# A diffusion trunk's modulation products in eight pair steps, and two of four value bands loaded later

## Chip, core and metric

The kernel runs on one core of a Trainium2 chip. The metric is device time in microseconds (us) of one execution; lower is better. Three runs of the kernel before gave a median of 1276.81 us (1274.63 to 1281.95). Engines are called as the profile calls them: PE (TensorE matmul; PEld is its weight load), DVE (VectorE), ACT (ScalarE), POOL (GpSimd) and SP (SyncE), whose queue issues every DMA of this kernel, in program order.

## What is computed

Two layers over 1152 tokens (128 context, 1024 latent on a 16 x 64 grid), width 1024. Each layer normalizes, modulates by a shift and a scale, mixes, and adds the result back through a gate:

```python
x = x + gate * mixer(rmsnorm(x) * (1 + scale) + shift)
(shift, scale, gate) = silu(cond) @ w_mod[l] + b_mod[l]
```

The even layer's mixer is a gated linear recurrence (HGRN2, 4 heads) beside a neighbourhood attention (8 heads of width 64, window 8 x 16, a relative bias, and all context keys); the odd layer's is a convolution with a gated recurrence. The change concerns the middle of the even layer: the projections that make keys, queries and gates of the attention, beside which the kernel computes the modulation rows that are needed later (layer 0's gate, layer 1's shift, scale and gate).

## The kernel before

Weights and activations are float32, split into a high and a low fp32r part; a product is three matmuls (high x high, low x high, high x low).

**Units.** `unit_f(i, c)` multiplies weight block `i` (128 output columns) by chunk `c` (384 tokens): 8 x 3 = 24 matmuls (L316 to L318) into one PSUM tile. The attention's projections (the loop over `p`, `n`, `c` at the end of the listing) are 12 weight blocks, block 3p + n, with three units each: **units 0 to 35**, block b being units 3b to 3b + 2. For n = 0 a unit's result goes to the keys, for n = 1 to the queries (tile `kq`), for n = 2 to the gate (`yT`). ACT copies each out of PSUM (helper `act`, L77), the gate with a DVE step behind it (L365). PSUM tag `mm` has three buffers, so unit u + 3 can't start before unit u's tile has been read.

**Weights.** `w_get(i, 0, 1)` splits block `i + 1` while block `i` is used: the load `wraw` (512 KB), its high part on ACT (`wh`, 1.06 us), its low part on POOL (`wl`, L186). A `wh` stands in ACT's order between two units' copies: while it waits for its load, the copies behind it wait as well.

**Modulation.** The later modulation is two groups of 8 blocks of k. One block is 1 MB of `w_mod` (two tiles `wm`) and four matmuls (L221), one for each column group of 32, that accumulate into one PSUM tile. After the 8th block DVE adds the bias row (`modR`, L227); `mod_done` transposes it (L234), sets the factors and stores the gate row (`gate_d`).

**What sets the order.** `at(u, f, ...)` puts a call on an agenda, and `tick()`, called after each unit, runs what stands there for that unit. Tile's scheduler then makes each engine's order from priorities and free buffers. Large tiles (`wm`, `wraw`, `wh`, `wl`, `kq`, `vband`, ...) share 20 buffers of one pool, `slab`. A load is issued when SP comes to it, its buffer is free, and the load eight places before it on SP has landed.

**Bands.** The values were stored to `vb_d` in DRAM before the stage. `band_load(Rg)` brings four grid rows back as keys for the attention: four loads `vband` of 256 KB whose access pattern has 4 as its outermost size. Bands 0 to 2 are read by the first half's items, bands 1 to 3 by the second's. Behind the bands SP issues six masks (`mkt`), the cached keys and values (`kc`, `vc`) and the biases (`bT`, outermost size 8); POOL and DVE subtract a bias from a mask (`nbm`, L822), and the first score of the attention (PE L845, then DVE L852) needs the first of these.

Of the kernel before, what the change touches and what calls it, by code (L numbers as in the profile page):

```python
# [33 lines left out]
def trunk_kernel(ctx: ExitStack, tc: tile.TileContext, x, wm0, wm, bmr, wfe, wv, woe, wfo, woo, rgw, sm, st0,  # L34
# [12 lines left out]
    def slab(name, shape=(128, T), dt=F32):  # L47
        return sp.tile(list(shape), dt, name=name, tag="slab")
# [3 lines left out]
    def psum(tag, shape=(128, 512)):  # L52
        return pp.tile(list(shape), F32, name="ps_" + tag, tag=tag, bufs=PB[tag])

    def load(out, in_):
        return nc.sync.dma_start(out=out, in_=in_)
# [139 lines left out]
    def w_get(i, la_load, la_split):  # L196
        w_split(i)
        w_split(i + la_split)
        w_load(i + la_load)
        return split[i]  # L200


    rows = {}

    def mod_load(g, ks):
        for k in ks:
            for hf in range(2):
                t = slab("wm", (128, 1024))
                load(t, wm[g - 1, k, :, hf * 1024:(hf + 1) * 1024])
                rows[g, k, hf] = t  # L210

    def mod_row(g):
        t = slab("bmrow", (128, 512))
        ap = bass.AP(tensor=bmr.tensor, offset=bmr.offset + g * 2048, ap=[[512, 4], [0, 32], [1, 512]])
        load(t, ap)
        return t

    def mod_mm(g, ps, ks):
        for k in ks:
            for b in range(4):  # L220
                PE.matmul(ps[32 * b:32 * b + 32, :], condS[:, k, :],  # L221
                          rows[g, k, b // 2][:, (b % 2) * 512:(b % 2 + 1) * 512],
                          start=(k == 0), stop=(k == 7), skip_group_check=True)

    def mod_evac(g, ps, bm):
        R = slab("modR", (128, 512))
        V.tensor_tensor(R, ps, bm, OP.add)  # L227
        return R
# [118 lines left out]
    def at(u, f, *a):  # L347
        agenda.setdefault(u, []).append((f, a))
# [359 lines left out]
    def vb_unit(b, t):  # L708
        o = unit_v(IVB + 2 * b, t)
        if t == 0:  # L710
            dst = vbc[:, b * 256:(b + 1) * 256]
        else:
            if (t - 1) // 2 not in vbt:
                vbt[(t - 1) // 2] = slab("vbt", (128, 2, 512))
            dst = vbt[(t - 1) // 2][:, (t - 1) % 2, b * 256:(b + 1) * 256]
        with tc.high_priority(200):
            act(dst, o, AF.Copy)
        tick()

    def band_store(Rg):  # L720
        store(vb_d[2 * Rg:2 * Rg + 2].rearrange("t p f -> p t f"), vbt.pop(Rg))
# [10 lines left out]
    for b in range(2):  # L732
        w_get(IVB + 2 * b + 1, 2, 1)
        for t in range(9):
            if b == 1 and t in (2, 5, 8):
                mod_load(1, [t // 3])
            vb_unit(b, t)
            if t == 5:
                w_get(IVB + 2 * b + 1, 2, 2)
            if b == 1 and t in (2, 4, 6, 8):  # L740
                band_store(t // 2 - 1)
        split.pop(IVB + 2 * b)
        split.pop(IVB + 2 * b + 1)
# [2 lines left out]

    mst = {}

    MODS = [(g, k) for g in (1, 2) for k in range(8)]

    def mod_step(n):
        g, k = MODS[n]
        if k == 0:
            mst["ps"] = psum("a")
        mod_mm(g, mst["ps"], [k])
        rows.pop((g, k, 0))
        rows.pop((g, k, 1))
        if n + 3 < len(MODS):
            mod_load(MODS[n + 3][0], [MODS[n + 3][1]])
        if k == 7:  # L760
            mst[g] = mod_evac(g, mst["ps"], mod_row(g))

    def mod_done(g):
# [148 lines left out]
            V.tensor_tensor(yT[4 + p, 0][:, 0:128], o[:, 0:128], yT[4 + p, 0][:, 0:128], OP.mult)  # L912

    U = clock["u"]
    for n in range(16):
        at(U + 4 + n, mod_step, n)
        if n % 8 == 7:
            at(U + 4 + n + 1, mod_done, MODS[n][0])
    for Rg in range(4):
        at(U + 20 + 3 * Rg, band_load, Rg)  # L920
    for p in range(4):
        for n in range(3):
            i = IP + 3 * p + n
# [30 lines left out]
    for i in range(n_it + 3):  # L954
        if 0 <= i - 2 < n_it:
            a_trans(i - 2)
        if i < n_it:
            a_score(i)
            p, hf, j = items[i]
# [23 lines left out]
    def out_tiles(i0, ts, last=8, cuts=HALVES):  # L983

        ps = {t: [psum("o" if n == 1 and p else "mm") for p in cuts[:-1]] for n, t in enumerate(ts)}
        for ks in (range(last), range(last, 8)):
            for t in ts:
                c, tt = divmod(t, 3)
                z = slice(tt * 128, (tt + 1) * 128)
                for o, p, q in zip(ps[t], cuts, cuts[1:]):  # L990
                    for k in ks:
                        yh, yl = ysp[k, c]
                        wh, wl = split[i0 + k]
                        PE.matmul(o[:, :q - p], yh[:, z], wh[:, p:q], start=(k == 0), stop=False)  # L994
                        PE.matmul(o[:, :q - p], yh[:, z], wl[:, p:q], start=False, stop=False)  # L995
                        PE.matmul(o[:, :q - p], yl[:, z], wh[:, p:q], start=False, stop=(k == 7))  # L996
        return ps
# [19 lines left out]
    for t in range(9):  # L1017
        xt = slab("xt", (128, 1024))
        load(xt, x[t])
        ps = out_tiles(IWE, [t])[t]  # L1020
# [195 lines left out]
    for pos in range(max(ev) + 1):  # L1216
# [6 lines left out]
        n, c = seq[pos]  # L1223
# [14 lines left out]
    for t in range(9):  # L1238
# [3 lines left out]
        ps = pst[t] if t < 2 else out_tiles(IWO, [t], 8, cuts)[t]  # L1242
# [128 lines left out]
```

## Time and profile before

| | us |
|---|---|
| median of three runs | 1276.81 |
| the profiled execution's own time | 1281.0 |
| its span | 1279.2 |
| PE busy | 1204.3 (94%) |
| DVE busy | 680.5 (53%) |
| ACT busy | 529.2 (41%) |
| POOL busy | 349.1 (27%) |

PE is busy nearly throughout, so a gap on PE or a stretch at a lower clock is what lengthens the span; the other engines matter where PE waits for them. The profile lists for a stretch the busy time of each engine, the clock granted to PE (1.00 is 2.4 GHz, 0.50 is 1.2 GHz), the mean busy share of the 16 DMA engines and GB/s; in a timeline, `[4.21 <-DVE yT L365]` is idle time before an instruction and what ended it. The profiled execution is 4.2 us above the median.

### The profile page before, as it was taken

To read this page: it belongs to the slowest core of one execution; us is meant where nothing else is said; L and a number is where in the kernel's file an instruction comes from. 1 tells how busy PE (TensorE), PEld (TensorE's weight loads), DVE (VectorE), ACT (ScalarE), POOL (GpSimd) and SP (SyncE) were. 2 spreads that over 40 slices of the span, in tenths; PEclk is the share of its full clock that TensorE was granted. 3 is DMA by queue.
4 is the path that set the end of the run, shared out by engine and by line. 5 is a ranking of instruction groups with operands and counts; after the bars stand their busy time and mean duration, and the time that the engine had idled before them with its cause. 6 is when DMAs were issued, how large, how long until landed. Compare 5 with 4: busy or idle time off the path is not lost. (4 is left out here: it accounts for less than half of the span.)

```text
span 1279.2 us, 19143 instructions
## 1 busy us (share of the span) xinstructions
PE 1204.3 (94%) x7536; PEld 1082.4 (85%) x7536; DVE 680.5 (53%) x1424; ACT 529.2 (41%) x1057; POOL 349.1 (27%) x261
## 2 busy tenths in 40 slices
PE   5999998999999999998999999999988999898897
PEld 3889998999999997787956667888988999897686
DVE  5547128314555200000168996654678779888744
ACT  3435134323343211111146674323477586574311
POOL 0142032421505110111150420025444435442000
PEclk9999999999998999998969999999989999999899
DMA  9510100111010446522430224223011111112432
GB/s 349 194 34 22 34 17 26 36 52 37 18 40 25 155 165 210 199 84 100 128 120 2 98 83 181 99 100 132 17 34 46 46 28 39 42 53 64 139 124 83
DMA packets 41909, 110.45 MB, mean 86 GB/s; under 512 B 4180, under 2 KB 14804, under 8 KB 41820
## 3 DMA queue, kind: packets, MB, share of 16 engines
q1 hardware_dynamic: 41820, 109.24, 25.1%
q8 instruction: 59, 0.97, 0.3%
q14 instruction: 30, 0.25, 0.1%
HBM read 96.61 MB, written 12.61 MB: 85 GB/s over the span
## 5 line engine op out<-in xcount | busy, mean ns | idle before, releaser
L316 PE MATMUL ps_mm<-hTh,wh 128*128 128x384 f32 x936 | 320.1, 346 | 11.2 <-DVE yT L365 4.2
L317 PE MATMUL ps_mm<-hTl,wh 128*128 128x384 f32 x936 | 319.8, 342 | 2.3 <-DVE hTl L307 1.7
L318 PE MATMUL ps_mm<-hTh,wl 128*128 128x384 f32 x936 | 319.9, 342 | 1.0 <-POOL wl L186 1.0
L186 POOL TENSOR_TENSOR wl<-wraw,wh 128x1024 fp32r<-128x1024 f32 x48 | 123.5, 2574 | 285.9 <-ACT wh L77 251.1
L316 PEld LDWEIGHTS ps_mm<-hTh,wh 128*128 128x128 f32 x936 | 177.6, 191 | 27.4 <-ACT kq L77 7.0
L317 PEld LDWEIGHTS ps_mm<-hTl,wh 128*128 128x128 f32 x936 | 178.4, 191 | 4.6 <-DVE hTl L307 3.3
L318 PEld LDWEIGHTS ps_mm<-hTh,wl 128*128 128x128 f32 x936 | 178.4, 191 | 1.8 <-POOL wl L186 1.6
L994 PE MATMUL ps_mm<-wh,yh 128*128 128x512 f32 (+1 forms) x288 | 112.8, 393 | 6.1 <-ACT yh L77 5.8
L995 PE MATMUL ps_mm<-wl,yh 128*128 128x512 f32 (+1 forms) x288 | 113.1, 393 | 2.0 <-DVE wl L186 2.0
L996 PE MATMUL ps_mm<-wh,yl 128*128 128x512 f32 (+1 forms) x288 | 112.5, 391 | 1.7 <-DVE yl L977 1.7
L77 ACT ACTIVATE wh<-wraw 128x1024 fp32r<-128x1024 f32 x68 | 71.4, 1057 | 86.5 <-DMA wraw<-in_wfe_dram 39.7
L339 PE MATMUL ps_mm<-wh,hTh 128*128 128x256 f32 x288 | 83.2, 289 | 2.0 <-ACT va L77 2.0
L341 PE MATMUL ps_mm<-wh,hTl 128*128 128x256 f32 x288 | 81.9, 284 | 0.0
L340 PE MATMUL ps_mm<-wl,hTh 128*128 128x256 f32 x288 | 81.8, 284 | 0.0
L262 POOL TENSOR_TENSOR ss<-ss,nhalf 128x1 f32<-128x1 f32 x27 | 15.2, 564 | 243.8 <-DVE ss L261 186.2
L1127 POOL TENSOR_TENSOR yT<-yT,rt 128x384 f32<-128x384 f32 x42 | 56.8, 1382 | 72.2 <-DVE rt L1124 72.2
L77 ACT ACTIVATE res<-xt 128x512 f32<-128x512 f32 (+1 forms) x37 | 22.9, 619 | 124.9 <-DVE xt L1004 117.0
L994 PEld LDWEIGHTS ps_mm<-wh,yh 128*128 128x128 f32 x288 | 54.6, 190 | 18.6 <-ACT yh L77 6.3
L822 POOL TENSOR_TENSOR nbm<-mkt,bT 128x384 f32<-128x384 f32 x42 | 44.8, 1084 | 86.9 <-DMA bT<-in_bias_dram 51.7
L995 PEld LDWEIGHTS ps_mm<-wl,yh 128*128 128x128 f32 x288 | 54.5, 189 | 15.8 <-DVE wl L186 4.1
L996 PEld LDWEIGHTS ps_mm<-wh,yl 128*128 128x128 f32 x288 | 54.5, 189 | 13.7 <-DVE yl L977 2.3
L365 DVE SCALAR_TENSOR_TENSOR yT<-yT,ps_mm 128x384 f32<-128x384 f32 x10 | 5.5, 554 | 113.2 <-ACT yT L77 113.2
(258 smaller groups left out, 2458.5 us busy)
## 6 DMA issues: line engine op xcount, KB each, us to landing
wm<-in_wm_dram SPq DMA_DIRECT2D x48, 512.0 KB
wraw<-in_wfe_dram SPq DMA_DIRECT2D x28, 512.0 KB
xt<-in_x_dram SPq DMA_DIRECT2D x18, 512.0 KB
bT<-in_bias_dram SPq DMA_DIRECT2D x48, 192.0 KB
wraw<-in_wfo_dram SPq DMA_DIRECT2D x16, 512.0 KB
x_d<-xt SPq DMA_DIRECT2D x9, 512.0 KB
xt<-x_d SPq DMA_DIRECT2D x9, 512.0 KB
out_dram<-xt SPq DMA_DIRECT2D x18, 256.0 KB
```

The lines of the kernel that those rows point to most:

```text
L77: i = A.activation(out, in_, func, **kw)
L186: (lo_eng or G).tensor_tensor(lo, r, hi.bitcast(F32), OP.subtract)
L316: PE.matmul(o, w1, hh, start=(k == 0), stop=False)
L317: PE.matmul(o, w1, hl, start=False, stop=False)
L318: PE.matmul(o, w2, hh, start=False, stop=(k == 7))
L339: PE.matmul(o, hh, w1, start=(k == 0), stop=False)
L340: PE.matmul(o, hh, w2, start=False, stop=False)
L341: PE.matmul(o, hl, w1, start=False, stop=(k == 7))
L994: PE.matmul(o[:, :q - p], yh[:, z], wh[:, p:q], start=(k == 0), stop=False)
L995: PE.matmul(o[:, :q - p], yh[:, z], wl[:, p:q], start=False, stop=False)
L996: PE.matmul(o[:, :q - p], yl[:, z], wh[:, p:q], start=False, stop=(k == 7))
L1127: G.tensor_tensor(us[c], us[c], r[:, c * CW:(c + 1) * CW], OP.mult)
```

## The change

The 16 steps of one block become 8 steps of two blocks, at every second unit from unit 4 on (4, 6, ..., 18) in place of every unit from 4 to 19. Loads run two pairs ahead (8 `wm` tiles) where they ran three blocks ahead (6 tiles), so four blocks, not three, are loaded before the stage. `mod_done` of the second group comes one unit earlier. Bands 2 and 3 are put on the agenda at units 33 and 34 in place of 26 and 29; bands 0 and 1 stay at 20 and 23.

```diff
@@ -732,8 +732,8 @@
-            if b == 1 and t in (2, 5, 8):
-                mod_load(1, [t // 3])
+            if b == 1 and t in (2, 4, 6, 8):
+                mod_load(1, [t // 2 - 1])
@@ -746,18 +746,19 @@
-    MODS = [(g, k) for g in (1, 2) for k in range(8)]
+    MODS = [(g, (k, k + 1)) for g in (1, 2) for k in (0, 2, 4, 6)]
 
     def mod_step(n):
-        g, k = MODS[n]
-        if k == 0:
+        g, ks = MODS[n]
+        if n % 4 == 0:
             mst["ps"] = psum("a")
-        mod_mm(g, mst["ps"], [k])
-        rows.pop((g, k, 0))
-        rows.pop((g, k, 1))
-        if n + 3 < len(MODS):
-            mod_load(MODS[n + 3][0], [MODS[n + 3][1]])
-        if k == 7:
+        mod_mm(g, mst["ps"], ks)
+        for k in ks:
+            for hf in range(2):
+                rows.pop((g, k, hf))
+        if n + 2 < len(MODS):
+            mod_load(*MODS[n + 2])
+        if n % 4 == 3:
             mst[g] = mod_evac(g, mst["ps"], mod_row(g))
@@ -912,12 +913,12 @@
-    for n in range(16):
-        at(U + 4 + n, mod_step, n)
-        if n % 8 == 7:
-            at(U + 4 + n + 1, mod_done, MODS[n][0])
+    for n in range(8):
+        at(U + 4 + 2 * n, mod_step, n)
+        if n % 4 == 3:
+            at(U + 4 + 2 * n + 1, mod_done, MODS[n][0])
     for Rg in range(4):
-        at(U + 20 + 3 * Rg, band_load, Rg)
+        at(U + (20, 23, 33, 34)[Rg], band_load, Rg)
```

Three places show how the scheduler's order moves.

PE, behind unit 4, the first step. Before:

```order
L317 MATMUL ps_mm<-hTl,wh 128x384
L318 MATMUL ps_mm<-hTh,wl 128x384
L221 MATMUL ps_a<-wm,condS 32x512 x4
L316 MATMUL ps_mm<-hTh,wh 128x384
L317 MATMUL ps_mm<-hTl,wh 128x384
```

and now:

```order
L317 MATMUL ps_mm<-hTl,wh 128x384
L318 MATMUL ps_mm<-hTh,wl 128x384
L221 MATMUL ps_a<-wm,condS 32x512 x8
L316 MATMUL ps_mm<-hTh,wh 128x384
L317 MATMUL ps_mm<-hTl,wh 128x384
```

The four matmuls of the second block have come up from behind unit 5 and stand directly behind those of the first; the same at the other seven steps.

SP, from the weights of block 8 to the first masks (the difference; `out_dram<-kq` are the stores of the new keys of p = 2 and p = 3):

```order
+L59 DMA out_dram<-kq 128x128
 L56 DMA wraw<-in_wfe_dram 128x1024
 L56 DMA vband<-vb_d 128x1x512 x4
-L56 DMA wraw<-in_wfe_dram 128x1024
-L56 DMA vband<-vb_d 128x1x512 x4
-L56 DMA wraw<-in_wfe_dram 128x1024
-L56 DMA vband<-vb_d 128x1x512 x4
+L56 DMA wraw<-in_wfe_dram 128x1024 x3
 L59 DMA out_dram<-kq 128x128
-L56 DMA wraw<-in_wfe_dram 128x1024
+L56 DMA vband<-vb_d 128x1x512 x8
 L56 DMA mkt<-in_msk_dram 128x384 x6
```

The loads of blocks 9, 10 and 11 now stand together behind band 1; bands 2 and 3 stand behind them and behind the store of p = 3's keys (unit 27), directly ahead of the masks. In the program's text the bands are called at units 33 and 34; in SP's order nothing of unit 28 or later stands ahead of them.

ACT, units 20 to 30, from the keys' last copy of p = 2 on. Before:

```order
L77 ACTIVATE kq<-ps_mm 128x384 x3
L77 ACTIVATE wh<-wraw 128x1024
L77 ACTIVATE kq<-ps_mm 128x128
L77 ACTIVATE kq<-ps_mm 128x4x4x16 x2
L77 ACTIVATE kq<-ps_mm 128x2x4x16
L77 ACTIVATE wh<-wraw 128x1024
L77 ACTIVATE kq<-ps_mm 128x6x4x16
L77 ACTIVATE yT<-ps_mm 128x384
L77 ACTIVATE wh<-wraw 128x1024
L77 ACTIVATE yT<-ps_mm 128x384 x2
```

and now:

```order
L77 ACTIVATE kq<-ps_mm 128x384 x2
L77 ACTIVATE wh<-wraw 128x1024
L77 ACTIVATE kq<-ps_mm 128x384
L77 ACTIVATE kq<-ps_mm 128x128
L77 ACTIVATE kq<-ps_mm 128x4x4x16 x2
L77 ACTIVATE kq<-ps_mm 128x2x4x16
L77 ACTIVATE wh<-wraw 128x1024
L77 ACTIVATE kq<-ps_mm 128x6x4x16
L77 ACTIVATE wh<-wraw 128x1024
L77 ACTIVATE yT<-ps_mm 128x384 x3
```

The high part of block 8 has moved ahead of unit 20's copy (it stood behind it), that of block 9 stays between the copies of units 22 and 23, and that of block 10 has moved from behind unit 24's copy to ahead of it.

## Rows read from the trace of the kernel before

**Rows 1.** The page's first line: the profiled execution.

```profile
span 1279.2 us, 19143 instructions
```

**Rows 2.** Stretches: length; busy PE, PEld, DVE, ACT, POOL (instructions); granted clock, DMA share, GB/s.

```profile
475.56:557.81 82.25, 82.25 (x493) 65.15 (x492) 4.19 (x8) 12.77 (x24) 12.02 (x5) 1.00 0.51 172
557.81:594.28 36.47, 34.55 (x200) 33.71 (x196) 1.48 (x4) 4.24 (x9) 4.80 (x2) 1.00 0.36 119
594.28:598.66 4.38, 0.17 (x1) 0.00 (x0) 0.61 (x2) 2.07 (x4) 0.94 (x1) 0.91 0.09 36
598.66:605.69 7.03, 7.03 (x24) 7.03 (x25) 0.41 (x1) 0.12 (x1) 1.47 (x1) 0.57 0.18 58
```

**Rows 3.** Waits of PE, 560 to 606 us: total, times, longest.

```profile
PE ps_mm L316 <- DVE yT L365: 4.2, 1, 4.2
PE ps_mm L316 <- ACT kq L77: 1.6, 1, 1.6
PE ps_mm L318 <- POOL wl L186: 0.3, 1, 0.3
```

**Rows 4.** Timeline of SP's queue: start, duration of the issue, DMA.

```profile
559.31 1.71 SPq L56 DMA_DIRECT2D vband<-vb_d  x3
561.12 0.62 SPq L56 DMA_DIRECT2D wraw<-in_wfe_dram  x1
...
571.32 0.90 SPq L56 DMA_DIRECT2D wraw<-in_wfe_dram  x1
...
583.58 2.40 SPq L56 DMA_DIRECT2D wraw<-in_wfe_dram  x1
600.15 2.58 SPq L56 DMA_DIRECT2D vband<-vb_d  x4
...
605.52 19.10 SPq L56 DMA_DIRECT2D mkt<-in_msk_dram  x6
...
629.11 10.88 SPq L56 DMA_DIRECT2D bT<-in_bias_dram  x14
```

**Rows 5.** Timeline of ACT: start, duration, instruction [idle before, what ended it].

```profile
572.21 1.06 ACT L77 ACTIVATE wh<-wraw 128x1024 fp32r<-128x1024 f32 x1 [9.44 <-DMA wraw<-in_wfe_dram]
...
584.31 1.06 ACT L77 ACTIVATE wh<-wraw 128x1024 fp32r<-128x1024 f32 x1 [10.16 <-issue]
...
596.59 1.06 ACT L77 ACTIVATE wh<-wraw 128x1024 fp32r<-128x1024 f32 x1 [10.46 <-DMA wraw<-in_wfe_dram]
```

**Rows 6.** Timeline of PE: two steps and the unit between; a unit without one.

```profile
475.56 1.07 PE L221 MATMUL ps_a<-wm,condS 128*32 128x512 f32 x8
...
476.01 0.61 PE L221 MATMUL ps_a<-wm,condS 128*32 128x512 f32 x4
476.55 0.45 PE L316 MATMUL ps_mm<-hTh,wh 128*128 128x384 f32 x1
...
481.95 0.45 PE L316 MATMUL ps_mm<-hTh,wh 128*128 128x384 f32 x1
...
605.69 0.34 PE L316 MATMUL ps_mm<-hTh,wh 128*128 128x384 f32 x1
...
609.85 0.34 PE L316 MATMUL ps_mm<-hTh,wh 128*128 128x384 f32 x1
```

**Rows 7.** A stretch in which band loads alone move (columns as in rows 2).

```profile
576.00:584.00 8.00, 8.00 (x46) 7.87 (x46) 0.00 (x0) 0.00 (x0) 0.00 (x0) 1.00 0.26 102
```

**Rows 8.** The attention's start: three timelines (POOL, PE, DVE), then two stretches.

```profile
633.44 1.01 POOL L822 TENSOR_TENSOR nbm<-mkt,bT 128x384 f32<-128x384 f32 x1 [13.39 <-PE ps_b L318]
...
634.90 0.92 PE L845 MATMUL ps_mm<-kq 64*128 64x384 f32 x4
...
636.52 0.63 DVE L852 CUSTOM_DVE_ANT_0 ps_mm<-ps_mm,nbm,nm 128x384 f32<-128x384 f32 x1
...
637.00:642.50 5.50, 3.17 (x13) 2.08 (x14) 5.27 (x19) 2.71 (x8) 2.65 (x4) 0.98 0.53 199
642.50:662.50 20.00, 20.00 (x76) 11.55 (x76) 11.32 (x30) 7.81 (x19) 15.65 (x15) 0.50 0.39 143
```

## Prediction, written before the changed kernel ran

> **What bounds the kernel now.** I read the page first: PE is busy 94% of a span of 1279.2 us [rows 1], so I looked for what PE loses in the stage that the change touches. The stretches of that stage come next [rows 2]. From the first modulation step to unit 20 (475.56 to 557.81) PE has no gap and the full clock: there only PE's own work counts, and a load that comes a little earlier or later is worth nothing. From 557.81 to 605.69 it is otherwise. PE's waits there [rows 3] are 4.2 us for unit 25's gate (unit 28 needs its PSUM buffer), 1.6 us for unit 23's copy and 0.3 us for a low part. Behind the 4.2 us the clock falls to 1.2 GHz: one unit takes 7.03 us, at a mean clock of 0.57 [rows 2], where a unit at full clock takes 609.85 - 605.69 = 4.16 us [rows 6].
>
> All three waits have one cause. ACT stands idle 9.4, 10.2 and 10.5 us for the weights of blocks 8, 9 and 10 [rows 5], with the units' copies behind it. Those loads are issued at 561.12, 571.32 and 583.58 [rows 4] and are used at 572.2, 584.3 and 596.6: 11 to 13 us each. In between SP issues band after band. Where bands alone move, the DMA engines' mean share is 0.26, at 102 GB/s [rows 7]: four engines of sixteen. One band load of 256 KB takes these four 256 KB / 102 GB/s = 2.57 us, a band of four loads 10.3 us, and a weight load behind a band waits with its share on these engines.
>
> **The sum, part by part.**
>
> *Pair steps.* Each program matmul of a step shows as two records: eight records in two rounds of four. A round lasts 476.01 - 475.56 = 0.45 us [rows 6], where the x4 row is the second round alone. A unit with a step takes 481.95 - 476.55 = 5.40 us, so a step costs 5.40 - 4.16 = 1.24 us, of which 0.90 is streaming and 0.34 entry and exit (a late start and a slow first matmul behind it). A pair enters once: eight entries fewer are 8 x 0.34 = 2.7 us on PE, which bounds this stretch. No row shows two blocks in one go. The bounds are 0 and 2.7; I take 2.7, since a third round can follow the second as the second follows the first. Bytes and matmuls stay the same.
>
> *The loads of `wm`.* Four blocks are ahead in place of three, and a pair is loaded two steps ahead, which is four units and more: some 20 us for 2 MB, in a stretch that moves 172 GB/s [rows 2], so that 2 MB take 12 us. Cost 0. If that cover went, each step would wait for the rest.
>
> *Blocks 8 to 10.* The last step now stands behind unit 18, so the gate store and the rest of band 0 come one unit earlier, and bands 2 and 3 no longer stand between the weight loads. I lay the new times out from unit 20, which starts 2.7 us earlier and behind the second group's transposes (0.4 us, which stood behind it): 557.8 - 2.7 + 0.4 = 555.5. Unit 19 then starts at 550.9. Block 8's load was issued 3.3 us behind the last step; with the key store ahead of it on SP that makes 554.7, and with the 11.1 us of before it is used at 565.8. Unit 20's copy, now behind it on ACT, is done by 567.4; unit 23, which needs that buffer, starts at 555.5 + 3 x 4.16 = 568.0. The margin is 0.6 us. Block 9's load moves as far, to 577.9; unit 23's copy is done at 579.5, and unit 26 starts at 580.5: margin 1.0 us, where 1.6 us were lost. Block 10's load now follows directly; unit 24's gate is out by some 581.5, unit 27 starts at 584.6. So the waits of 6.1 us go, and with them the slow unit, 7.03 - 4.16 = 2.9 us: **9.0 us** [rows 2, 3]. As a check: from unit 20 to the first score are 634.90 - 557.81 = 77.1 us [rows 8], and sixteen units take 66.6; 10.5 are lost, of which 0.4 are transposes. The bounds of this term are 10.1 (all of it) and about 5 (both thin margins missed by some 2 us).
>
> *Bands 2 and 3.* Who waits for them next: the masks and biases behind them on SP, and the attention's first score behind those. SP issues the bands when it has passed the store of unit 27's keys, at about 589.3, and when there are buffers; the last four loads use tiles of block 9, free behind unit 29, at 597.1. Eight loads take 20.6 us: with 1.5 us to land they are done between 611.4 (all from 589.3 on) and 619.2 (all from 597.1 on). Before, four masks and all that follows waited for unit 33 anyway [rows 4], so the issue of the six masks takes 19.10 us there; the first bias was issued at 629.11, 6.7 us behind that unit's start (634.90 - 3 x 4.16 = 622.4). Now unit 33 starts at 609.6, and the first bias could go at 616.3. From it to the first finished mask were 5.3 us (633.44 + 1.01), and DVE wanted that at 636.52: 2.1 us of slack [rows 8]. So the bands must be done by 618.4; of the interval 611.4 to 619.2 nearly all is early enough. Cost 0 to 1, taken as 0.
>
> Sum: 2.7 + 9.0 = 11.7 us, which makes 1281.0 - 11.7 = 1269.3 us of the profiled execution. That execution is 4.2 us above the median of the runs; against the median it is 1276.8 - 11.7 = **1265.1 us** (-0.9%). Behind the stage all follows from the attention's start, so the gain should be carried to the end.
>
> **A rule against it.** The row shows four busy engines under the bands [rows 7] and 0.53 under the biases [rows 8], some eight. The Trainium skill (DMA: Bandwidth & Descriptors, the sections on queues and rings and on why a DMA increments its semaphore by 16) says that the outermost size sets how many engines a load uses, that these are the lowest-numbered ones, and that each engine takes its ring in order; by it the biases can't pass the bands, and bands held until unit 33 would cost the time of the second rival below. The trace agrees on the shares; which engines they are it doesn't say.
>
> **Rivals.**
>
> *The weights stay late.* Bands 0 and 1 still stand around blocks 8 and 9, and the margins are 0.6 and 1.0 us. With both loads 2 us later than I have them, 2.4 us of waits come back, and a half-clock stretch perhaps: gain 5 to 9, 1268 to 1272 us. For it: 11 to 13 us a load are from another mix. Against it: fewer bands stand ahead.
>
> *The attention starts late (the other side).* If the bands are issued only at unit 33, where the text calls them, they are done at 609.6 + 20.6 + 1.5 = 631.7, the first bias goes 15.4 us later than 616.3, and less the slack PE stands idle 13.3 us. Net loss 1.6, and 2.9 for the unit at half clock behind such a gap: 1278 to 1282 us. It decides at 618.4. For it: SP takes its queue in order, and the bands stand directly ahead of the masks. Against it: nothing later than unit 27 stands ahead of them, and the buffers are free by unit 29.
>
> *Another clock at the attention's start.* PE was at 0.50 for 20.0 us there, behind a thin stretch (3.17 us busy in 5.5) [rows 8]. If that fall doesn't come, DVE bounds the stretch (11.3 us busy of 20; at the 5.27 of 5.5 just before, 11.8 us): 8.2 us more gain, 1257 us. If it lasts longer, as much less: up to 1273. Nothing in the change aims at it, but the start shifts against the clock's own rhythm.
>
> *Nothing changes in effect.* If the weights had waited for buffers and not for bands, only the 2.7 us would come: 1274. The issue times [rows 4] speak against it: SP had issued each load 11 us and more before ACT could use it.
>
> **How the numbers follow.** A difference under 0.5% (6.4 us) can't be told from none by a measurement of this kernel. Chances: the sum as it stands 0.66 (1263 to 1269, all of it faster), weights late 0.14 (0.08 faster, 0.06 the same), attention late 0.09 (0.06 slower, 0.03 the same), the clock 0.08 (half faster, half the same), no effect 0.03 (the same). That makes faster 0.78, same 0.16, slower 0.06. The range leaves out the late attention and the farthest of the clock's gain: 1259 to 1273.
>
> **What would show it.** Right: a pair step of about 2.1 us (four rounds); PE without a gap over 0.5 us from unit 20 to unit 35, at clock 1.00; the first score some 77 - 10 = 67 us behind unit 20; block 8 to 10's `wh` earlier than 566, 578 and 580; band 3 landed by 615, the first bias issued within 7 us of unit 33's start. Wrong: a pair of 2.4 us; a gap before unit 23 or 26; an idle PE between the last unit and the first score; a slow stretch at the attention's start of another length than 20 us.

## The result, and the profile after

| | before | after |
|---|---|---|
| median, 20 runs each side by side | 1276.82 us | 1266.78 us |
| lowest to highest | 1274.43 to 1285.81 | 1261.57 to 1278.12 |
| ratio, 95% interval | | 0.9917 [0.9901, 0.9933] |
| the profiled execution's own time | 1281.0 | 1278.12 |

The changed kernel is 0.8% faster: 10.6 us by the ratio, 10.0 by the medians, where 11.7 us were forecast (1265.1 us). The execution that was profiled is the slowest of its 20, so its page misleads if one reads the top only. Its first line and the row of the granted clock (40 slices of 32 us):

```profile
span 1276.3 us, 19142 instructions
...
PEclk9999998799998999999969999999988999999899
```

The seventh and eighth slices (191 to 255 us) are low, in a part that the change does not touch. Stretches of the same trace (columns as in rows 2): that low part, the stage from the first modulation step to unit 20 and from there to the first score, and the stretch behind the attention's start.

```profile
213.00:241.00 28.00, 26.21 (x123) 26.24 (x124) 12.80 (x30) 4.00 (x18) 9.95 (x9) 0.52 0.00 1
484.56:564.46 79.90, 79.90 (x497) 66.61 (x497) 4.88 (x9) 12.56 (x24) 12.04 (x5) 1.00 0.52 171
564.46:632.17 67.71, 67.71 (x387) 67.45 (x385) 2.36 (x6) 10.92 (x23) 10.42 (x5) 1.00 0.39 122
...
637.00:657.50 20.50, 19.75 (x72) 11.29 (x72) 12.12 (x35) 7.79 (x19) 16.36 (x17) 0.50 0.49 179
```

How to read it: in the first row PE runs at half clock for 27 us and does 123 matmuls. Unit 0 starts at 462.32, where the trace of before has 453.32, so everything in this trace stands 9.0 us late before the stage begins. The stage itself took 82.25 + 77.09 us before ([rows 2, 8]: 475.56 to 557.81 to 634.90) and takes 79.90 + 67.71 now: 11.73 us less. The 9.0 us that this trace had lost ahead of it hide most of that: the two spans differ by 2.9 us only. From unit 20 to the first score PE is busy for 67.71 of 67.71 us at clock 1.00; the view of PE's waits of that stretch has no row at all, where [rows 3] had three.

SP's queue (start, duration of the issue, DMA), the counterpart of [rows 4]:

```profile
560.76 0.56 SPq L59 DMA_DIRECT2D gate_d<-modR  x2
561.38 1.72 SPq L56 DMA_DIRECT2D vband<-vb_d  x3
...
564.01 0.37 SPq L56 DMA_DIRECT2D wraw<-in_wfe_dram  x1
564.47 8.93 SPq L56 DMA_DIRECT2D vband<-vb_d  x4
573.50 8.57 SPq L56 DMA_DIRECT2D wraw<-in_wfe_dram  x3
598.99 0.34 SPq L59 DMA_DIRECT2D out_dram<-kq  x1
599.43 12.61 SPq L56 DMA_DIRECT2D vband<-vb_d  x8
612.09 9.49 SPq L56 DMA_DIRECT2D mkt<-in_msk_dram  x6
621.67 4.90 SPq L56 DMA_DIRECT2D kc<-in_kct_dram  x4
...
627.68 32.28 SPq L56 DMA_DIRECT2D bT<-in_bias_dram  x26
```

Bands 2 and 3 (x8) go out from 599.43 on, behind unit 27's key store; the first is some 20 us ahead of unit 33, the last, at 609.57, some 10, although the program calls them at units 33 and 34. ACT's order, the counterpart of [rows 5]:

```profile
574.70 1.06 ACT L77 ACTIVATE wh<-wraw 128x1024 fp32r<-128x1024 f32 x1 [9.90 <-DMA wraw<-in_wfe_dram]
575.66 0.91 ACT L77 ACTIVATE kq<-ps_mm 128x384 f32<-128x384 f32 x3
...
588.03 1.06 ACT L77 ACTIVATE wh<-wraw 128x1024 fp32r<-128x1024 f32 x1 [10.03 <-DMA wraw<-in_wfe_dram]
589.00 0.47 ACT L77 ACTIVATE kq<-ps_mm 128x384 f32<-128x384 f32 x1
589.37 1.05 ACT L77 ACTIVATE wh<-wraw 128x1024 fp32r<-128x1024 f32 x1
```

ACT still stands idle 9.9 and 10.0 us for the weights of blocks 8 and 9, as before; what is new is that it no longer matters. Unit 23's copy ends at 589.47, and unit 26, which needs that buffer, starts at 589.83: 0.36 us to spare. Block 10's high part follows without a wait. The biases' start:

```profile
631.30 1.02 POOL L823 TENSOR_TENSOR nbm<-mkt,bT 128x384 f32<-128x384 f32 x1 [28.87 <-PE ps_b L318]
...
632.17 0.92 PE L846 MATMUL ps_mm<-kq 64*128 64x384 f32 x4
...
633.79 0.62 DVE L853 CUSTOM_DVE_ANT_0 ps_mm<-ps_mm,nbm,nm 128x384 f32<-128x384 f32 x1
```

The first finished mask is there at 632.32, and DVE wants it at 633.79: 1.5 us of slack, where there were 2.1 [rows 8].

### The profile page after: what moved, and what is told of

Read it like the earlier page. It is cut to its first block, busy times and chain, and to the rows that moved or that the text cites. A ratio compares the mean times of both kernels' runs of the same rounds, so it can differ in the third digit from the quotient of the medians.

```text
span 1276.3 us, 19142 instructions
## 1 busy us (share of the span) xinstructions
PE 1208.2 (95%) x7536; PEld 1091.1 (85%) x7536; DVE 679.1 (53%) x1424; ACT 530.2 (42%) x1057; POOL 349.8 (27%) x261
## 5 line engine op out<-in xcount | busy, mean ns | idle before, releaser
L996 PEld LDWEIGHTS ps_mm<-wl,yh 128*128 128x128 f32 x288 | 54.8, 190 | 15.8 <-DVE wl L186 4.1
```

## The experiments

Twelve more runs were made; 7 and 12 repeat the changed kernel and kernel 6. All ratios are to the kernel before, on the same chip. Not all rows come from the same chip, so rows are compared by their ratios or by their stretches, and medians of two rows only roughly. "To unit 20" is the stretch from the first modulation step to unit 20, "to the score" that from unit 20 to the first score, "attention" that from the first score to the first output product, each from the profile of one execution; "slow" is the length of the stretch at 1.2 GHz that begins 5 to 11 us behind the first score (kernel 5: 4.6). Each of these four columns shows a single execution. Kernels 6 and 7 have 3.4 us more at 1.2 GHz, 32 and 36 us behind the first score.

| kernel | median us | ratio, 95% | to unit 20 | to the score | attention | slow |
|---|---|---|---|---|---|---|
| before | 1276.8 | | 82.25 | 77.09 | 136.66 | 20 |
| changed | 1266.8 | 0.9917 [0.9901, 0.9933] | 79.90 | 67.71 | 135.23 | 20 |
| 1 pairs alone | 1269.2 | 0.9948 [0.9926, 0.9970] | 79.91 | 73.45 | 134.28 | 14 |
| 2 bands alone | 1273.9 | 0.9969 [0.9948, 0.9991] | 82.26 | 72.36 | 134.97 | 14 |
| 3 before, bands by rows | 1272.9 | 0.9972 [0.9957, 0.9988] | 82.26 | 74.75 | 136.90 | 20 |
| 4 changed, bands by rows | 1282.5 | 1.0018 [0.9991, 1.0046] | 79.90 | 70.59 | 138.07 | 20 |
| 5 all bands late | 1287.8 | 1.0071 [1.0047, 1.0094] | 79.90 | 67.45 | 156.74 | 41 |
| 6 changed, repeats 2 and 1 | 1259.0 | 0.9847 [0.9825, 0.9869] | 79.90 | 67.72 | 129.73 | 0 |
| 7 changed again | 1265.8 (one) | | 79.91 | 67.71 | 136.81 | 14 |
| 8 singles early, bands late | 1268.2 | 0.9920 [0.9900, 0.9941] | (a unit longer) | 67.58 | 135.29 | 14 |
| 9 before, repeats 2 and 1 | 1268.5 | 0.9959 [0.9936, 0.9982] | 82.25 | 76.98 | 129.44 | 10 |
| 10 changed, one repeat | 1271.9 | 0.9958 [0.9930, 0.9986] | 79.91 | 67.99 | 141.69 | 31 |
| 11 changed, repeats 3, 2, 1 | 1260.3 | 0.9882 [0.9860, 0.9905] | 79.90 | 67.71 | 130.40 | 7 |
| 12 as 6, again | 1258.0 | 0.9861 [0.9837, 0.9885] | 79.90 | 67.71 | 126.77 | 0 |

### The two halves of the change (1 and 2)

Kernel 1 is the changed kernel with the bands at their old units:

```diff
-        at(U + (20, 23, 33, 34)[Rg], band_load, Rg)
+        at(U + 20 + 3 * Rg, band_load, Rg)
```

> The changed kernel with the bands where they were before (bands 2 and 3 called at units 26 and 29): the pair steps alone. Theory: the pairs give their 2.4 us between the first step and unit 20 (79.9 us in place of 82.25) and nothing behind it; weight loads of blocks 9 and 10 stand behind bands again, so units 20 to 35 lose the waits and the half-clock unit again (unit 20 to first score about 77 us). Total -2 to -3 us against the kernel before, ratio about 0.998. Rival (the earlier place of block 8's load, which the pairs bring, is what removes the stalls): -9 us or more, ratio 0.992 to 0.993.

Kernel 2 is the kernel before with the opposite of that edit, and steps of one block.

> The kernel before with single steps, and bands 2 and 3 called at units 33 and 34: the move of the bands alone. Theory: first step to unit 20 stays at 82.3 us; the waits of units 25 to 28 and the half-clock unit go, so unit 20 to first score about 68 us; total -8 to -9.5 us, ratio about 0.993. Rival (both parts are needed, since block 8's load comes later without the pairs): a gap before unit 23 stays and the gain is 3 to 6 us, ratio 0.995 to 0.998.

Neither did what its theory said. The pairs gave more than their 2.4 us, 6.6 by the ratio, and the bands less than their 9, 4.0 by the ratio, which is what their rival had, except that unit 26 waits and not unit 23. PE's waits from 552 to 640 us say where each stops; first the pairs alone, then the bands alone (the attention's own waits are left out):

```profile
PE ps_mm L316 <- DVE yT L365: 3.2, 1, 3.2
...
PE ps_mm L316 <- ACT kq L77: 0.5, 1, 0.5
```

```profile
PE ps_mm L316 <- ACT kq L77: 2.6, 1, 2.6
...
PE ps_mm L318 <- POOL wl L186: 0.3, 1, 0.3
```

With the pairs alone the wait of 1.6 us for unit 23's copy [rows 3] shrinks to nothing and that for the gate of 4.2 to 3.2, because block 8's load goes out one unit earlier, and with it those behind it; a wait of 0.5 comes for unit 29's copy, which stands behind block 11's high part. With the bands alone it is the other way round: the gate's wait goes, and the wait for unit 23's copy stays, since block 9's load still stands behind band 1 and the late end of the steps. It grows from 1.6 to 2.6: block 9's weights are issued at 567.37 and used at 581.67, 14.3 us later, where they took 13.0 before. Why they took longer was not tried. A half-clock stretch of 3.4 us follows in either (6.8 before). In the stage the pairs are worth 2.34 + 3.64 = 6.0 us, the bands 4.7, both together 11.7, which is 1.0 more than the sum of the two.

### What the pairs did behind unit 20 (8)

Kernel 8 has the bands late and steps of one block, each a unit earlier:

```diff
-        at(U + 4 + n, mod_step, n)
+        at(U + 3 + n, mod_step, n)
         if n % 8 == 7:
-            at(U + 4 + n + 1, mod_done, MODS[n][0])
+            at(U + 3 + n + 1, mod_done, MODS[n][0])
```

> Single steps, but each one unit earlier (units 3 to 18), and bands 2 and 3 called at units 33 and 34: without pairs, the second group's end stands where the pairs put it. Theory (what the pairs did to units 20 to 35 is only that the last step, the gate store and band 0 come one unit earlier, so that blocks 8 and 9 do too): unit 20 to first score 68 us with no gap over 0.5 us, as in the changed kernel, and no gain in the steps themselves: -8 to -10 us against the kernel before, ratio 0.992 to 0.994. Rival (the 2.4 us that the pairs save before unit 20, or another order of the loads, is needed): gaps as with the bands alone, -4 us, ratio about 0.997.

The theory holds. From unit 20 to the first score PE is busy without a gap, as in the changed kernel:

```profile
554.92:622.50 67.58, 67.58 (x387) 67.33 (x385) 2.37 (x6) 10.91 (x23) 10.61 (x5) 1.00 0.39 122
```

So what the pairs bring behind unit 20 is the earlier end of the steps, not the pairing: with the bands late and the steps ending behind unit 18, all of the 9.4 us come; with the bands alone, half. (That the 3.6 us of kernel 1 are this too, with the bands at their old place, is inferred.) The pairing itself is seen in the stage only. From unit 0 to the first score the kernel before takes 181.58 us, kernel 8 172.67, the changed kernel 169.85: the pairs save 2.8 us. The times can't tell the two apart, 0.9920 against 0.9917, with intervals of 0.2% to either side.

### Do four DMA engines make the weights late? (3 and 4)

Both load a band tile as four DMAs of 32 partitions, in place of two whose outermost size is 4. That makes 32 band loads in place of 16, not the same number, as the expectation of kernel 3 has it. Kernel 3 does it in the kernel before, kernel 4 in the changed one:

```diff
-            for jj in range(2):
-                load(t[:, jj, :], bass.AP(tensor=v0.tensor, offset=v0.offset + BS[2 * jp + jj] * 512,
-                                          ap=[[64 * 512, 4], [512, 32], [1, 512]]))
+            for r in range(4):
+                load(t[32 * r:32 * r + 32], bass.AP(tensor=v0.tensor, offset=v0.offset + (64 * r + BS[2 * jp]) * 512,
+                                                    ap=[[512, 32], [(BS[2 * jp + 1] - BS[2 * jp]) * 512, 2], [1, 512]]))
```

> The kernel before, order and places untouched, but each band tile loaded as four DMAs of 32 partitions (outermost size 32) in place of two with outermost size 4: same bytes, same number of DMAs. Theory (the weight loads are late because the bands sit on four of sixteen DMA engines): the mean DMA share where bands alone move rises from 0.26 to near 1.0, the weights' high parts of blocks 8 to 10 no longer make units wait, and unit 20 to first score falls to 68 us with the bands at their old place: -8 to -9.5 us, ratio about 0.993. Rival (the weights wait for their place in SP's order or for buffers): the share rises but the gaps of 4.2 and 1.6 us stay, ratio 0.998 to 1.000.

> The changed kernel with each band tile loaded as four DMAs of 32 partitions (outermost size 32). Theory: units 20 to 35 already run without a gap there, so no more is to be had from the weights; the cached keys behind the bands no longer wait 3.3 us, but the first score waits for other things: within 2 us of the changed kernel, ratio to the kernel before 0.990 to 0.993. Rival (the first bias, behind the bands, sets the attention's start, or the start's slow stretch): 3 us and more better than the changed kernel, ratio 0.989 or less.

Kernel 3's engines under bands and block 8's weights (a stretch), then SP's issue of these weights, then ACT:

```profile
556.85:566.43 9.58, 9.58 (x59) 9.54 (x58) 0.24 (x2) 0.49 (x1) 0.00 (x0) 1.00 0.87 214
```

```profile
560.08 0.37 SPq L56 DMA_DIRECT2D wraw<-in_wfe_dram  x1
...
566.88 0.35 SPq L56 DMA_DIRECT2D wraw<-in_wfe_dram  x1
```

```profile
566.57 1.06 ACT L77 ACTIVATE wh<-wraw 128x1024 fp32r<-128x1024 f32 x1 [6.24 <-DMA vband<-vb_d]
...
586.45 0.49 ACT L77 ACTIVATE yT<-ps_mm 128x384 f32<-128x384 f32 x1 [3.72 <-PE ps_mm L318]
586.84 2.00 ACT L77 ACTIVATE wh<-wraw 128x1024 fp32r<-128x1024 f32 x2
```

The first half of the theory holds. The share is 0.87 at 214 GB/s, where bands alone had 0.26 at 102 [rows 7]. That stretch holds a weight load too; like for like, from the issue of block 8's weights to their use, the share was 0.41 before (561.12 to 572.21) and is 1.00 here. These weights are used 566.57 - 560.08 = 6.5 us behind their issue, not 11. (ACT's row names a band: it is the load eight places behind these weights, issued at 566.42, when they had landed.) By the Trainium skill (DMA: Bandwidth & Descriptors, the section on why a DMA increments its semaphore by 16) an outermost size of 32 puts a load on all sixteen engines and one of 4 on four; the shares of 0.26 and 0.87 agree with that.

The second half doesn't come: the scheduler now set the high parts of blocks 9 and 10 behind three gate copies. Block 9's, issued at 566.88, is split at 586.84, with no DMA named as its wait, and unit 27 waits 1.5 us for it and 1.7 for its low part. The edit changed more than the engines, and only they were meant: the number of loads, ACT's order, and PE's order too. One head's score product was set into the stage, ahead of unit 24 in kernel 3 (572.66, 0.84 us) and of unit 27 in kernel 4 (593.33, 0.91 us); for these two kernels "to the score" ends at the main group of score products, so it holds that early one, which the others have behind it. So kernel 3 gains 3.2 us like for like, and the 9 us of the theory are neither shown nor refuted.

Kernel 4 shows the same order on ACT, with gaps of 0.7 and 1.1 us; with the 0.9 us of the product they are most of the 2.9 us that it loses in the stage. Its last eight band loads stand among the first biases besides (from 628.27 on). Both expectations of kernel 4 failed: it is some 13 us slower than the changed kernel by the ratio. In the profiled execution 12.1 us lie ahead of unit 0, which starts at 461.56 and in kernel 7 at 449.48, and 2.9 in the stage. Its time fell in two groups (five runs of 1272.9 to 1275.7, six of 1282.0 to 1286.2 and one of 1293.8); the profiled one has the half-clock stretch from 213 to 241 us that the changed kernel's profile had. Why that stretch, far ahead of the edit, came in so many of its runs stays open.

### Is that stretch the change's? (7)

> The changed kernel once more, for the profile of another execution. Its profiled execution was the slowest of its runs: 27 us at half clock lay at 214 to 241 us, in a part that the change doesn't touch. Theory: this is of that execution alone; here the stage from the first modulation step to the first score takes 147.6 us again (before: 159.3), the stretch at 214 us is absent or 3 to 7 us long, and the time is 1262 to 1270 us. Rival (the change brings that stretch with it): it is there again and the time is about 1277.

The theory holds in this execution. Its stretches (the early part; the two of the stage; the one behind the attention's start):

```profile
213.00:241.00 28.00, 27.17 (x224) 27.03 (x225) 14.11 (x31) 7.27 (x28) 15.71 (x11) 1.00 0.11 31
471.72:551.63 79.91, 79.91 (x498) 66.62 (x497) 4.89 (x9) 12.56 (x24) 12.01 (x5) 1.00 0.52 170
551.63:619.34 67.71, 67.71 (x388) 67.45 (x386) 2.37 (x6) 10.90 (x23) 10.51 (x5) 1.00 0.39 122
625.00:638.60 13.60, 13.01 (x42) 7.23 (x41) 7.69 (x25) 5.73 (x14) 9.54 (x10) 0.51 0.53 196
```

The early part does 224 matmuls in 28 us at full clock, and the stage is the same to 0.01 us. What differs from execution to execution lies outside the stage: unit 0 starts at 449.48 here. The order of instructions speaks for it as well: in the traces of the changed kernel and of the kernel before every engine's order is the same up to 459 us of the former, so nothing that the change moved stands ahead of that stretch. The stretch behind the score is 13.6 us here and 20 in the first profile, and its length too belongs to the execution.

### The rival on the other side (5)

```diff
-        at(U + (20, 23, 33, 34)[Rg], band_load, Rg)
+        at(U + (33, 33, 34, 34)[Rg], band_load, Rg)
```

> The changed kernel with all four bands held back (called at units 33, 33, 34 and 34), so that 16 band loads stand between the last weights and the masks. Theory (the second rival of the prediction is a true mechanism, and the changed kernel stays clear of it because its 8 loads end in time): at 2.57 us a load the 16 take 41 us; issued from about unit 27's end (598 us in the trace of the changed kernel) they land by about 641, the first bias is issued some 17 us later than there, and the first score or the first softmax waits 10 to 15 us, with a stretch at half clock behind it: 8 to 18 us slower than the changed kernel, ratio to the kernel before 0.998 to 1.006. Rival (biases pass the bands, on other DMA engines or lanes): same as the changed kernel, 0.990 to 0.993.

SP's queue and PE at the attention's start:

```profile
587.92 33.40 SPq L56 DMA_DIRECT2D vband<-vb_d  x16
621.36 8.03 SPq L56 DMA_DIRECT2D mkt<-in_msk_dram  x6
632.08 3.92 SPq L56 DMA_DIRECT2D kc<-in_kct_dram  x4
...
637.17 3.42 SPq L56 DMA_DIRECT2D bT<-in_bias_dram  x5
```

```profile
620.35 0.92 PE L846 MATMUL ps_mm<-kq 64*128 64x384 f32 x4
637.92 0.80 PE L849 MATMUL ps_mm<-kc,kq 64*128 64x128 f32 x4 [16.66 <-DMA kc<-in_kct_dram]
```

The mechanism is real and larger than expected: 21 us over the changed kernel (1287.8 - 1266.8; 20 by the ratios), against 8 to 18. The first thing late is the cached keys, not the bias: SP issues them when the bands eight places ahead have landed. PE waits 16.7 us. The clock falls at 624.9, inside this wait, and stays at 1.2 GHz for 41 us, 28 of them behind the wait. Whether a bias can pass a band, the rule in the prediction, no run here shows: the first bias was issued at 637.17, and the last band had landed by 634.67, when the second load of cached keys, eight places behind it, went out. The same run shows the cover from the other side: with no band ahead of blocks 8 to 10 at all, the stage from unit 20 on takes 67.45 us. So of the changed kernel's 67.71 nothing over 0.3 us is left to take from the bands.

### Filling PE at the attention's start (6, 9, 10, 11, 12)

The one cost that the change left alone is the slow stretch behind the first score. Kernel 6 computes score products again over the same tile, before the softmax reads it:

```diff
+    FILL = {1: 2, 2: 1}
...
-            for e in range(2):
+            for e in [0, 1] * (1 + FILL.get(i, 0)):
                 o0 = 128 + hf * 512 + j * 128
...
                 PE.matmul(S[e][:, 0:384], lq, rk, start=True, stop=True)
```

> The changed kernel with score matmuls computed again over the same tiles before they are read: twice more in the second attention item, once more in the third, about 3 us of PE work in the stretch where PE waits for the first softmax. Theory (the clock falls at the attention's start because PE is thin there): the 20 us at 0.50 go or get shorter, 3 to 8 us less than the changed kernel, ratio to the kernel before 0.985 to 0.989. Rival (the fall comes whatever PE does there, or the repeats delay the softmax): the stretch stays at 20 us and the time is 0 to 3 us more than the changed kernel, ratio 0.991 to 0.995.

> The kernel with two and one repeats once more. With one repeat alone the stretch at half clock had grown to 31 us, though PE stood idle less than without repeats, so idle time alone doesn't decide whether the clock falls. Theory (the repeats' effect on the clock is a property of this kernel and not of one execution): no stretch over 7 us at half clock in the 35 us behind the first score, and a ratio of 0.983 to 0.988 again. Rival (it was luck of the executions seen so far): a stretch of 10 to 20 us, ratio 0.990 or more.

Kernel 9 does this to the kernel before; kernel 10 has `{1: 1}`, kernel 11 `{1: 3, 2: 2, 3: 1}`.

> The kernel before, its steps and bands untouched, with the repeated score matmuls of the second (twice) and third (once) attention items. Theory (what the repeats bring lies behind the first score, what the change brings lies ahead of it, so they add): first step to first score 159.3 us as before, no 20 us at half clock behind it, 7 to 9 us less than the kernel before, ratio 0.993 to 0.9945. Rival (the repeats only help where the stage ahead has had no slow stretch): 0.997 to 1.000.

> The changed kernel with the repeats cut to one, in the second item only (0.6 us of PE work in place of 1.6 us). Theory (thin PE is what brings the clock down): the gap behind the second item's scores is 0.5 us and the later ones stay, so part of the slow stretch stays (3 to 14 us) and the gain is between the two, ratio to the kernel before 0.986 to 0.990. Rival (not the clock but the new order of the attention's first items is what helps): the full gain, 0.984 to 0.986, with or without a slow stretch.

> The changed kernel with three, two and one repeats in the second, third and fourth items. Theory: nothing is left to win from the clock there, and the repeats begin to stand in the way of DVE's next item: 0 to 2 us more than with two and one, ratio to the kernel before 0.984 to 0.987. Rival (gaps of 2 us that remain still cost clock further on): less by 1 to 3 us, 0.982 to 0.984.

Kernel 6 is the fastest but for its own repetition: 1259.0 and 1258.0 us, 9 and 7 us less than the changed kernel by the ratios, with six extra matmuls. Two stretches of it behind the score, then the same two and the slow one of kernel 10, then 35 us of kernel 12:

```profile
620.05:622.80 2.75, 2.75 (x21) 1.84 (x22) 1.58 (x5) 0.42 (x1) 0.90 (x2) 1.00 0.47 168
622.80:625.30 2.50, 0.54 (x6) 0.22 (x4) 2.42 (x6) 1.14 (x4) 1.20 (x2) 1.00 0.53 197
```

```profile
623.85:626.50 2.65, 2.65 (x21) 1.68 (x20) 1.48 (x5) 0.32 (x1) 0.89 (x2) 1.00 0.52 180
626.50:629.00 2.50, 0.91 (x2) 0.29 (x2) 2.42 (x6) 1.24 (x4) 1.27 (x2) 0.98 0.53 200
629.00:660.00 31.00, 30.92 (x118) 18.32 (x120) 15.84 (x50) 11.61 (x27) 17.25 (x17) 0.51 0.35 125
```

```profile
621.26:656.26 35.00, 30.04 (x239) 19.77 (x238) 30.70 (x92) 19.61 (x48) 23.32 (x21) 1.00 0.44 141
```

In kernel 12 PE is busy 30.0 of 35 us at 2.4 GHz and DVE 30.7: neither is busy throughout, and PE no longer sets the pace alone. In kernel 10 PE is busy 30.9 of 31 us at 1.2 GHz while DVE has 15.8 us of work: PE limits, at half its clock. What makes the clock fall is not settled. The expected cause, idle time on PE, does not sort these runs: kernel 6 keeps its clock through 2.5 us with 0.54 us of PE work, and kernel 10 loses it for 31 us behind 2.5 us with 0.91. One repeat costs some 5 us against the changed kernel, two and one gain 8; the theory of kernel 10, a gain between none and that, failed, and so did its rival. Its profile is of one of its slowest executions (1275.08 us, median 1271.9), so 31 us may be more than it has as a rule. Kernel 11 bears its theory out in kind: nothing more to win (0.9882, just above the forecast 0.987; its interval overlaps that of kernel 12). On the kernel before the repeats are worth 5 us by the ratio, between theory and rival, with a slow stretch of 10 us left. Over all kernels but 5 the attention's length goes with the slow time: 127 to 130 us at 0 to 10, 134 to 138 at 14 to 20, 142 at 31. Inside the middle group it doesn't: the changed kernel's own two executions have 136.81 at 14 and 135.23 at 20. The repeats changed the order of the attention's first instructions too, and how much of the gain is order was not tried apart, so that the clock is the cause of it is argued and not shown.

## Why the prediction was right, step by step

*Pair steps, 2.7 us.* Right. Two rows of PE in the changed kernel:

```profile
484.56 1.92 PE L221 MATMUL ps_a<-wm,condS 128*32 128x512 f32 x16
...
495.04 1.92 PE L221 MATMUL ps_a<-wm,condS 128*32 128x512 f32 x16
```

From one pair to the next, with two units between, are 10.48 us, where two units with a step each took 10.80 [rows 6]: 0.32 us saved per pair. Less two units of 4.16 a pair costs 2.16 us (forecast: about 2.1). Over the stretch it is 82.25 - 79.90 = 2.35 us with the transposes, 0.35 us, moved in: 2.7 again. Loads of `wm` cost nothing: PE is busy for all 79.90 us.

*Blocks 8 to 10, 9.0 us.* Right in sum: 77.09 - 67.71 = 9.4, of which 0.35 are the transposes that moved out: 9.0. The timeline under it can be compared after taking off the 9.0 us that the whole trace stands late. Block 8's high part then starts at 565.7 (forecast 565.8), block 9's at 579.0 (577.9), block 10's at 580.4. Block 9 was 1.1 us later than laid out. Its load was issued at 573.50, which is 564.5 on the same clock and 6.8 us earlier than before, but was used 14.5 us behind its issue and not 13.0: that a load takes as long as before was the weak step. The margin of unit 26 was 0.36 us, not 1.0 (unit 23's was 1.1, forecast 0.6); that it held was partly luck. Two of the prediction's own signs, block 9's high part ahead of 578 and block 10's ahead of 580, just failed. What the prediction did not separate is who brings this term. It is filed under the moved bands and the earlier last step together, and kernels 1, 2 and 8 show that it needs both: of the 9.4 us, with the transposes, 3.6 come with the pairs alone, 4.7 with the bands alone, and the rest only with both.

*Bands 2 and 3, cost 0 to 1.* Right in cost, a little early in time. The last band landed by 616.3 on the same clock, when the second load of cached keys, which waits for it, was issued at 625.29 (forecast 611.4 to 619.2, wanted by 618.4, and to be seen by 615). The first bias was issued 8.4 us behind unit 33's start and not within 7. That used 0.6 of the 2.1 us of slack.

*Against the median.* 1276.8 - 11.7 = 1265.1 us; measured 1266.8, and 1265.8 in the repeated profile. By the ratio's interval the gain is 8.6 to 12.6 us, so 11.7 lies inside it. The attention and what follows carried the gain on: from the first score to the end both first profiles have the same length to 0.2 us (644.3 us before).

*The rivals.* The weights stayed late in kernels 1 and 2, each with a half of the change, and not in the changed kernel. The late attention came in kernel 5, when the bands were made late. The other clock came in part at most (20 us again in the first profile, 14 in the second, with no shorter attention). Kernels 6 and 12, without that stretch, are 9 and 7 us faster, which is in line with its price of 8.2, as far as the gain is not the new order.

## What to carry over

Read a stall by the queue behind it. Here three waits of PE, and the half-clock unit that followed, came from one engine order in which a split that waits for a weight load stands ahead of the copies that free PSUM; moving eight loads that nobody needed yet and ending a side job one unit sooner removed 4.7 and 3.6 of the 9.4 us by themselves, and all of it together. A late transfer is free until the next queue behind it runs out of slack, and that point can be worked out beforehand (618.4 here): eight loads stayed clear of it, sixteen cost 21 us. And a gain in a stage must be read in that stage: the first profile's span showed 2.9 us of the 11.7, because a slow stretch far ahead of it fell into that execution.

## What was not expected

- A few repeated matmuls where PE waits made the attention's start 5 to 10 us shorter, but only in some amounts: in the changed kernel three pairs of repeats (kernels 6 and 12) left no slow stretch there in the executions profiled, one pair left 31 us of it, none 14 to 20; in the kernel before three pairs left 10. PE's idle time just before does not tell which it will be.
- Once PE is at 1.2 GHz there, it stays busy without a gap (30.92 of 31.00 us) and still at the low level; a fully busy PE did not end the stretch at once.
- Loading the bands on more DMA engines made the weights land in 6.5 us in place of 11, and still gave only 2.3 us of the stage; the scheduler had changed ACT's and PE's order along with it.
- The half-clock stretch from 213 to 241 us came in one of 20 runs of the changed kernel as far as its times tell (1278.12 us, the next 1270.59), and by the same sign in half of kernel 4's, whose instructions up to there are in the same order. What sets it off stays open.
